# A hybrid block on one core: preparing the gate/up weights inside the output projection, and moving its token scale, its squares and the buffers of the down projection

## The chip, the core and the metric

One program runs on one core of a Trainium2 chip. The metric is device time in microseconds (us) of one execution, as a median of three. The engines named here are TensorE (PE in the profile), VectorE (DVE), ScalarE (ACT), GpSimd (POOL) and SyncE (SP), which issues most transfers (DMA). PSUM is the memory into which matmuls write; SBUF holds everything else.

## The reference

For 512 tokens, a model width of 2048 and an inner width of 5632 (all float32):

```
mod = silu(c) @ w_ada + b_ada -> sh1, sc1, g1, sh2, sc2, g2
u   = rmsnorm(h) * norm_attn * (1 + sc1) + sh1
y   = concat(FoX heads, NSA heads)(u @ w_in) @ w_out     # mixer
h   = h + g1 * y
u   = rmsnorm(h) * norm_ffn * (1 + sc2) + sh2
h   = h + g2 * ((silu(u @ w_gate) * (u @ w_up)) @ w_down)
out = rmsnorm(h) * final_norm
```

The change touches the end of `@ w_out`, the second norm, the start of gate/up, the passage to `@ w_down`, and the last norm.

## The kernel before, in words

The hidden state stays transposed: 16 tiles `hT` of 128 features x 512 tokens. Every large product is computed from split operands. A raw weight `wr` is rounded to `wh` on ACT (L239), the rest `wl` is formed on DVE (L240), and PE adds three matmuls, high x high, low x high and high x low (L255 to L257). One `gemm` goes through its weights in chunks `ct` and calls a `hook(ct)` after the matmuls of each chunk.

The output projection runs in groups of feature tiles; the last two are tiles 10 to 13 and tiles 14 and 15. The latter has eight chunks of 12 matmuls. After a group, `res_add` forms `hT` on DVE (L1006), ACT squares it (L997), POOL adds the squares up (L999), and `sum_rstd` sums over the features with 128x1 matmuls on PE (L821): of the running sum `hsum` and of the last two squares. `rstd_of` makes the inverse root on DVE and ACT; `rows_of` spreads it over the partitions with four matmuls (L173), and ACT copies the result into the SBUF tile `rb` (L175).

Gate and up together are 176 steps `s` (22 groups of 8 steps). A step multiplies seven combinations of two activation tiles with seven of the weights, in 42 matmuls of 128x256 into seven PSUM banks `y`. For its weights it needs `raw` (two loads on SP), the sums `sum` (DVE), and the splits `hx`/`lx` and `hs`/`ls`: `hx`, `hs` and a first form of `lx` on ACT, `ls` on DVE, while the second half of `lx` is an adding transfer that POOL issues (L1039). For its activations, in the first eight steps alone, DVE scales two `hT` tiles by the norm (`u_raw`, L1053, with `rb`), DVE or POOL takes differences (`u_mix`, L1059 to L1062), ACT rounds (`uh`), and DVE forms the rests (`ul`, L1076 and L1079). After a group, `evac` combines the seven banks on DVE (L1109 to L1115), and `glu` sends the product to DRAM (`hd`).

The down projection reads `hd` back (`hr`, L1254), splits it into `fh` (ACT) and `fl` (DVE, L1258), and runs four phases over the inner width, each of four groups of four feature tiles. Its SBUF pools lie over those of gate/up, so each tile waits until the old tiles at its address are dead. In the last phase the squares of the new `hT` (called `hU` there) are added up as above. The tail transposes `hU` (L1294), scales it into `ot` (L1297 and L1299), and stores it (L1300) from four buffers.

The order on each engine comes from a scheduler, except from the first `u_raw` to the last `evac`, where program order holds on every engine. Each engine works its queue in order, so an instruction that waits holds all behind it. SP always follows program order.

Of the kernel before, what the change touches and what calls it, by code (L numbers as in the profile page):

```python
# [13 lines left out]
OP = mybir.AluOpType  # L14
# [63 lines left out]
def hymba_block(ctx: ExitStack, tc: tile.TileContext, x, c, positions, w_ada, b_ada, norm_attn,  # L78
# [738 lines left out]
    def sum_rstd(tiles, n, tag, name):  # L817
        b = bank(tag)
        for i, a in enumerate(tiles):
            for t in range(NT):  # L820
                nc.tensor.matmul(b[:, t:t + 1], a[:, t * P:(t + 1) * P], one_col, start=i == 0 and t == 0,  # L821
                                 stop=i == len(tiles) - 1, skip_group_check=True)
        return rstd_of(b[:, 0:NT], n, name)
# [163 lines left out]
    pf = pool(wo, "pf")  # L987
# [3 lines left out]
    def add_sq(src, i, acc, name):  # L991
        if i == 0:
            acc.append(pf.tile([P, T], F32, tag="osum", name=name))
            nc.scalar.activation(acc[0], src, AF.Square)
            return
        sq = pf.tile([P, T], F32, tag="sq", name=uid("sq"), bufs=3)
        nc.scalar.activation(sq, src, AF.Square)  # L997
        if i < ND - 2:
            nc.gpsimd.tensor_tensor(acc[0], acc[0], sq, op=OP.add)  # L999
        else:  # L1000
            acc.append(sq)
# [34 lines left out]
    def x_low(s):  # L1036
        lx[s] = ring2.tile([P, 3, HT], F32R, tag="lx", name=uid("lx"), bufs=4)
        nc.scalar.activation(lx[s], raw[s][:, 1:4, :], AF.Copy, scale=-1.0)  # L1038
        nc.gpsimd.dma_start(split_ap(lx[s]), raw[s][:, 1:4, :], accum_op=OP.add)  # L1039

    def s_split(s):
        hs[s] = ring2.tile([P, 4, HT], F32R, tag="hs", name=uid("hs"), bufs=2)
        ls[s] = ring2.tile([P, 4, HT], F32R, tag="ls", name=uid("ls"), bufs=2)
        nc.scalar.copy(hs[s], sums[s])  # L1044
        nc.vector.tensor_tensor(ls[s], sums[s], split_ap(hs[s]), op=OP.subtract)  # L1045
# [80 lines left out]
    hsum = []  # L1126
    side_ada.extend(ada_block(pf, sec, j) for sec, j in todo_ada[9:])
    for i0, n, g in ((0, 4, g0), (4, 2, g1), (6, 4, BANKS_A), (10, 4, BANKS_B), (14, 2, BANKS_A)):
        k0 = 8 if i0 < 6 else 0
        if i0 >= 6:  # L1130
            g = out_group(i0, n, g)

        def x_hook(ct):
            if ct == k0 // 2 + 2:
                for i in range(i0, i0 + n):
                    nc.sync.dma_start(hT[i], xsp[i])

        gemm(*g, order=order, k0=k0, hook=x_hook, n_ada=1)
        res_add(i0, [o[3] for o in g[3]], 2, hsum, "hsum")
        for i in range(i0, i0 + n):  # L1140
            nc.gpsimd.dma_start(hsd[i], hT[i])
    pump(side_ada, 1000)
    for s in range(6):
        w_load(s)
# [3 lines left out]
    for s in range(2):  # L1148
        w_sums(s)
    for s in range(2):  # L1150
        x_high(s)
    rb = rows_of(sum_rstd(hsum, D, "mm", "rs2"), "mm", res.tile([P, T], F32, name="rb2"))
# [37 lines left out]

    u_raw(0)
# [3 lines left out]
    for s in range(3):  # L1195
        x_low(s)
    s_split(0)
# [42 lines left out]
    hp = pool(ft, "hp", reuse_waits="tile")  # L1240
    hT = [hp.tile([P, T], F32, name=f"hU{i}") for i in range(ND)]
# [3 lines left out]
    fsum = []  # L1245
# [6 lines left out]
    def h_tile(i):  # L1252
        r = pf.tile([P, T], F32, tag="hr", name=uid("hr"), bufs=4)
# [15 lines left out]
    for p, ph in enumerate(phases):  # L1269
# [3 lines left out]
        for g in range(4):  # L1273
            Z = banks4()

            def hook(ct):
                if p == 0 and ct == 2:
                    for i in range(4 * g, 4 * g + 4):
                        nc.sync.dma_start(hT[i], hsd[i])
                if nxt and (ct % 2 or nk < 12):  # L1280
                    b.append(h_tile(nxt.pop(0)))
# [5 lines left out]
    rf = sum_rstd(fsum, D, "mm", "rs3")  # L1287
    for i in range(ND):
        nc.scalar.activation(hT[i], hT[i], AF.Copy, scale=fin[:, i:i + 1])
    for t in range(NT):  # L1290
        for g in range(4):
# [3 lines left out]
            ot = pf.tile([P, T], F32, tag="hr", name=uid("ot"), bufs=4)  # L1295
# [31 lines left out]
```

## Time and profile before

| | before |
|---|---|
| median of 3 runs | 2497.86 us (2496.89 to 2498.45) |
| the profiled execution | 2492.28 us, of which the span is 2490.4 us |
| mean granted clock of TensorE | 0.969 of full |
| busy: PE, DVE, ACT, POOL | 94%, 66%, 42%, 18% |
| chain that ended last | PE 53%, DVE 1%, DMA 1% |

The profiled execution lies 5.6 us below the median of the runs, and 1.9 us of it lie outside the span. The rows below count from the start of the span. PE is busy nearly throughout; the stretches beside the change in which it isn't are the passage from the output projection to gate/up (from about 1046 us), the passage to the down projection (from about 1968 us), and the tail (from about 2468 us).

### The profile page before, as it was taken

The numbers are of one execution on the slowest core, as the hardware profiler recorded it, in microseconds if no ns is written. First come the engines' busy times: TensorE is split into PE (matmuls) and PEld (weight loads), VectorE is DVE, ScalarE is ACT, GpSimd is POOL, SyncE is SP. The second block draws the span as 40 slices with busy tenths as digits, with TensorE's granted clock in tenths as the row PEclk, the third lists the DMA queues.
The fourth block names the chain that finished last, engine by engine and source line by source line (L and its number), as shares of the span: only waits on it lengthen the run. The fifth ranks groups of instructions, "written<-read, shape, count | busy, mean of one in ns | idle before, by whom it ended". The sixth has DMA issues, their size and how long they took to land.

```text
span 2490.4 us, 38618 instructions
## 1 busy us (share of the span) xinstructions
PE 2336.9 (94%) x14643; PEld 2094.0 (84%) x14643; DVE 1633.2 (66%) x2757; ACT 1055.0 (42%) x1619; POOL 458.1 (18%) x468
## 2 busy tenths in 40 slices
PE   4688999999999989879999999999999799999998
PEld 3576888788887768769999999999999788888887
DVE  8995787887755565597777777777776533333333
ACT  4343643433423332355555555555555322222233
POOL 5564000200010221162221212222221100000011
PEclk7798999999999999989999999999999899999998
DMA  9782653453655267559898889898988454333322
GB/s 299 237 263 90 195 154 127 124 152 114 193 154 159 81 218 251 178 137 222 225 224 217 220 213 239 215 226 212 223 200 196 129 188 134 126 119 119 106 93 102
DMA packets 321690, 440.31 MB, mean 177 GB/s; under 512 B 25200, under 2 KB 216528, under 8 KB 321504
## 3 DMA queue, kind: packets, MB, share of 16 engines
q1 hardware_dynamic: 288080, 348.20, 43.4%
q0 software_dynamic: 31120, 85.45, 18.4%
q10 hardware_dynamic: 2304, 4.20, 0.4%
q8 instruction: 115, 1.88, 0.3%
q14 instruction: 71, 0.58, 0.1%
HBM read 340.18 MB, written 28.38 MB: 148 GB/s over the span
## 4 chain that ended last, share of the span: by engine, by line
PE 53%; DVE 1%; DMA 1%; ACT 0%; issue 0%; POOLq 0%; POOL 0%; SPq 0%; DVEq 0%; ACTq 0%
PE py L1096 11%; PE py L1099 11%; PE py L1098 11%; PE psmm L256 3%; PE psmm L257 3%; PE psmm L255 3%; PE pss L255 2%; PE pss L256 2%; PE pss L257 2%; PE pso L256 1%; PE pso L257 1%; PE pso L255 1%; DMA wr<-in_w_down_dram 0%; DMA out_dram<-ot 0%; DVE ot L1297 0%
## 5 line engine op out<-in xcount | busy, mean ns | idle before, releaser
L240 DVE TENSOR_TENSOR wl<-wr,wh 128x1024 fp32r<-128x1024 f32 (+2 forms) x194 | 219.5, 1132 | 366.9 <-ACT wh L239 365.2
L239 ACT CAST wh<-wr 128x1024 fp32r<-128x1024 f32 (+2 forms) x210 | 199.0, 948 | 514.4 <-PE psmm L256 212.7
L1099 PE MATMUL py<-uh,ls 128*128 128x256 f32 x1408 | 398.4, 283 | 3.0 <-DVE ls L1045 3.0
L1098 PE MATMUL py<-ul,hs 128*128 128x256 f32 x1408 | 399.0, 283 | 1.5 <-DVE ul L1079 1.5
L1096 PE MATMUL py<-uh,hs 128*128 128x256 f32 x1408 | 399.5, 284 | 1.0 <-DVE ev L1113 0.5
L1044 ACT CAST hs<-sum 128x1024 fp32r<-128x1024 f32 x176 | 184.5, 1048 | 383.5 <-PE py L1098 257.2
L1045 DVE TENSOR_TENSOR ls<-sum,hs 128x1024 fp32r<-128x1024 f32 x176 | 215.3, 1224 | 195.3 <-ACT hs L1044 195.3
L1098 PE MATMUL py<-ul,hx 128*128 128x256 f32 x1056 | 297.4, 282 | 8.3 <-DVE ul L1079 8.3
L1099 PE MATMUL py<-uh,lx 128*128 128x256 f32 x1056 | 298.0, 282 | 6.2 <-DMA lx<-raw 6.2
L1096 PE MATMUL py<-uh,hx 128*128 128x256 f32 x1056 | 299.3, 283 | 2.3 <-ACT uh L1078 2.0
L1099 PEld LDWEIGHTS py<-uh,ls 128*128 128x128 f32 x1408 | 269.0, 191 | 4.0 <-DVE ls L1045 3.8
L1096 PEld LDWEIGHTS py<-uh,hs 128*128 128x128 f32 x1408 | 268.3, 191 | 2.6 <-issue 0.7
L1098 PEld LDWEIGHTS py<-ul,hs 128*128 128x128 f32 x1408 | 268.4, 191 | 2.3 <-DVE ul L1079 2.3
L1039 POOL DMA_DIRECT2D lx<-raw x176 | 155.9, 891 | 552.8 <-ACT lx L1038 385.0
L1098 PEld LDWEIGHTS py<-ul,hx 128*128 128x128 f32 x1056 | 199.4, 189 | 9.4 <-DVE ul L1079 9.4
L1099 PEld LDWEIGHTS py<-uh,lx 128*128 128x128 f32 x1056 | 199.4, 189 | 6.5 <-DMA lx<-raw 6.5
L1096 PEld LDWEIGHTS py<-uh,hx 128*128 128x128 f32 x1056 | 200.3, 190 | 2.8 <-ACT uh L1078 2.3
L358 DVE SCALAR_TENSOR_TENSOR acc<-ad,sl,acc 128x512 f32<-128x512 f32 x180 | 140.0, 778 | 51.4 <-DMA ad<-in_w_ada_dram 49.8
L1038 ACT ACTIVATE lx<-raw 128x768 fp32r<-128x768 f32 x176 | 148.0, 842 | 0.0
L1034 ACT CAST hx<-raw 128x768 fp32r<-128x768 f32 x176 | 144.0, 818 | 1.7 <-DMA raw<-in_w_gate_dram 1.7
L255 PE MATMUL psmm<-fh,wh 128*128 128x512 f32 x352 | 136.9, 389 | 0.0
L256 PE MATMUL psmm<-fl,wh 128*128 128x512 f32 x352 | 136.9, 389 | 0.0
(438 smaller groups left out, 5481.3 us busy)
## 6 DMA issues: line engine op xcount, KB each, us to landing
ad<-in_w_ada_dram SPq DMA_DIRECT2D x192, 512.0 KB, 4.7
lx<-raw POOLq DMA_DIRECT2D x176, 384.0 KB, 4.9
raw<-in_w_up_dram SPq DMA_DIRECT2D x176, 256.0 KB, 4.1
raw<-in_w_gate_dram SPq DMA_DIRECT2D x176, 256.0 KB, 4.3
wr<-in_w_down_dram SPq DMA_DIRECT2D x88, 512.0 KB, 3.7
wr<-in_w_in_dram SPq DMA_DIRECT2D x104, 256.0 KB, 3.7
wr<-in_w_in_dram SPq DMA_DIRECT2D x24, 512.0 KB, 4.4
wr<-in_w_out_dram SPq DMA_DIRECT2D x24, 512.0 KB, 4.7
```

Source lines behind the costliest of these rows:

```text
L239: nc.scalar.copy(wh[:, :, s], v)
L240: lo.tensor_tensor(wl[:, :, s], v, split_ap(wh)[:, :, s], op=OP.subtract)
L255: nc.tensor.matmul(dst, wh[:, k, w], ah, start=first, stop=False)
L256: nc.tensor.matmul(dst, wh[:, k, w], al, start=False, stop=False)
L257: nc.tensor.matmul(dst, wl[:, k, w], ah, start=False, stop=last)
L1038: nc.scalar.activation(lx[s], raw[s][:, 1:4, :], AF.Copy, scale=-1.0)
L1039: nc.gpsimd.dma_start(split_ap(lx[s]), raw[s][:, 1:4, :], accum_op=OP.add)
L1044: nc.scalar.copy(hs[s], sums[s])
L1045: nc.vector.tensor_tensor(ls[s], sums[s], split_ap(hs[s]), op=OP.subtract)
L1096: nc.tensor.matmul(o, wh[:, wi, js], vh[:, vi, :], start=k == 0 and j == 0, stop=False, skip_group_check=True)
L1098: nc.tensor.matmul(o, wh[:, wi, js], vl[:, vi, :], start=False, stop=False, skip_group_check=True)
L1099: nc.tensor.matmul(o, wl[:, wi, js], vh[:, vi, :], start=False, stop=k == KG - 1, skip_group_check=True)
```

## The change

It has five parts. (a) The hook of the last `w_out` group issues the loads of the first six weight steps, the sums and `hx` of steps 0 and 1, `lx` of steps 0 to 2 and `hs` of step 0; `lx` and `hs` move to the pool `ring1`, which exists by then. (b) The spread token scale `rb` stays in a PSUM bank of gate/up, where `u_raw` reads it; the copy on ACT goes. (c) `s_split(0)`, which forms `ls` of step 0, stands ahead of `u_raw(0)`. (d) The tiles of the squares in the down stage move to the pool `hp`, and `hr` and `ot` have eight buffers for four; the addresses of the down stage's other buffers shift by this, over other tiles of gate/up. (e) POOL adds up fewer squares of the last norm (tiles 0 to 11 for 0 to 13); their sum goes to PE in the middle of the last group, and each remaining square has its own matmuls (`sum_tok`). For the second norm POOL's sum goes to PE inside the last group likewise.

```diff
@@ -814,8 +814,8 @@
                 nc.gpsimd.tensor_tensor(osum[grp][0], osum[grp][0], sq, op=OP.add)
         return f
 
-    def sum_rstd(tiles, n, tag, name):
-        b = bank(tag)
+    def sum_rstd(tiles, n, tag, name, b=None):
+        b = bank(tag) if b is None else b
         for i, a in enumerate(tiles):
             for t in range(NT):
                 nc.tensor.matmul(b[:, t:t + 1], a[:, t * P:(t + 1) * P], one_col, start=i == 0 and t == 0,
@@ -984,21 +984,26 @@
     rs = ExitStack()
     res = pool(rs, "res", side="right", reuse_waits="tile")
     wo = ExitStack()
-    pf = pool(wo, "pf")
+    pf = sqp = pool(wo, "pf")
     hT = [res.tile([P, T], F32, name=f"hT{i}") for i in range(ND)]
     hsd = [dram.tile([P, T], F32, name=f"hsd{i}") for i in range(ND)]
 
     def add_sq(src, i, acc, name):
         if i == 0:
-            acc.append(pf.tile([P, T], F32, tag="osum", name=name))
-            nc.scalar.activation(acc[0], src, AF.Square)
+            acc["t"] = sqp.tile([P, T], F32, tag="osum", name=name)
+            nc.scalar.activation(acc["t"], src, AF.Square)
             return
-        sq = pf.tile([P, T], F32, tag="sq", name=uid("sq"), bufs=3)
+        sq = sqp.tile([P, T], F32, tag="sq", name=uid("sq"), bufs=3)
         nc.scalar.activation(sq, src, AF.Square)
-        if i < ND - 2:
-            nc.gpsimd.tensor_tensor(acc[0], acc[0], sq, op=OP.add)
+        if i < acc["n"]:
+            nc.gpsimd.tensor_tensor(acc["t"], acc["t"], sq, op=OP.add)
         else:
-            acc.append(sq)
+            sum_tok(acc, sq, False, i == ND - 1)
+
+    def sum_tok(acc, a, first, last):
+        for t in range(NT):
+            nc.tensor.matmul(acc["b"][:, t:t + 1], a[:, t * P:(t + 1) * P], one_col, start=first and t == 0,
+                             stop=last, skip_group_check=True)
 
     def res_add(i0, Z, sec, acc, name):
         for m in range(len(Z)):
@@ -1034,14 +1039,18 @@
         nc.scalar.copy(hx[s], raw[s][:, 1:4, :])
 
     def x_low(s):
-        lx[s] = ring2.tile([P, 3, HT], F32R, tag="lx", name=uid("lx"), bufs=4)
+        lx[s] = ring1.tile([P, 3, HT], F32R, tag="lx", name=uid("lx"), bufs=4)
         nc.scalar.activation(lx[s], raw[s][:, 1:4, :], AF.Copy, scale=-1.0)
         nc.gpsimd.dma_start(split_ap(lx[s]), raw[s][:, 1:4, :], accum_op=OP.add)
 
+    def s_high(s):
+        hs[s] = ring1.tile([P, 4, HT], F32R, tag="hs", name=uid("hs"), bufs=2)
+        nc.scalar.copy(hs[s], sums[s])
+
     def s_split(s):
-        hs[s] = ring2.tile([P, 4, HT], F32R, tag="hs", name=uid("hs"), bufs=2)
+        if s not in hs:
+            s_high(s)
         ls[s] = ring2.tile([P, 4, HT], F32R, tag="ls", name=uid("ls"), bufs=2)
-        nc.scalar.copy(hs[s], sums[s])
         nc.vector.tensor_tensor(ls[s], sums[s], split_ap(hs[s]), op=OP.subtract)
 
     V, tmix, ur = {}, {}, {}
@@ -1123,7 +1132,7 @@
         nc.gpsimd.dma_start(hd[g][:, :, 0:HT], u1)
         nc.gpsimd.dma_start(hd[g][:, :, HT:], u2)
 
-    hsum = []
+    hsum = {"n": 14}
     side_ada.extend(ada_block(pf, sec, j) for sec, j in todo_ada[9:])
     for i0, n, g in ((0, 4, g0), (4, 2, g1), (6, 4, BANKS_A), (10, 4, BANKS_B), (14, 2, BANKS_A)):
         k0 = 8 if i0 < 6 else 0
@@ -1134,22 +1143,29 @@
             if ct == k0 // 2 + 2:
                 for i in range(i0, i0 + n):
                     nc.sync.dma_start(hT[i], xsp[i])
+            if i0 == 14:
+                if ct < 6:
+                    w_load(ct)
+                if ct == 2:
+                    hsum["b"] = bank("s")
+                    sum_tok(hsum, hsum["t"], True, False)
+                if 2 <= ct < 4:
+                    w_sums(ct - 2)
+                    x_high(ct - 2)
+                if 2 <= ct < 5:
+                    x_low(ct - 2)
+                if ct == 5:
+                    s_high(0)
 
         gemm(*g, order=order, k0=k0, hook=x_hook, n_ada=1)
         res_add(i0, [o[3] for o in g[3]], 2, hsum, "hsum")
         for i in range(i0, i0 + n):
             nc.gpsimd.dma_start(hsd[i], hT[i])
     pump(side_ada, 1000)
-    for s in range(6):
-        w_load(s)
     scale_vec(1, 0, ND)
     dsh = con.tile([P, KG], F32, name="dsh")
     nc.vector.tensor_tensor(dsh, mod[:, 3 * ND + KG:4 * ND], mod[:, 3 * ND:3 * ND + KG], op=OP.subtract)
-    for s in range(2):
-        w_sums(s)
-    for s in range(2):
-        x_high(s)
-    rb = rows_of(sum_rstd(hsum, D, "mm", "rs2"), "mm", res.tile([P, T], F32, name="rb2"))
+    r2 = rstd_of(hsum["b"][:, 0:NT], D, "rs2")
     pk.close()
     wo.close()
     aw.close()
@@ -1188,13 +1204,14 @@
         m0 = 5 * ND + 2 * j
         nc.vector.tensor_tensor(mod[:, m0:m0 + 2], b[:, 0:2], b_mod[:, m0:m0 + 2], op=OP.add)
 
+    rb = ps2.tile([P, T], F32, tag="y", name=uid("py"), bufs=8)
+    for t in range(NT):
+        nc.tensor.matmul(rb[:, t * P:(t + 1) * P], r2[:, t:t + 1].to_broadcast([P, P]), ident, start=True, stop=True)
+    s_split(0)
     u_raw(0)
     u_mix(0, nc.vector)
     u_raw(1)
     u_mix(1, nc.gpsimd)
-    for s in range(3):
-        x_low(s)
-    s_split(0)
     u_split(0)
     u_raw(2)
     late = []
@@ -1238,11 +1255,12 @@
     fs.close()
     ft = ExitStack()
     hp = pool(ft, "hp", reuse_waits="tile")
+    sqp = hp
     hT = [hp.tile([P, T], F32, name=f"hU{i}") for i in range(ND)]
     wts = pool(ft, "wts2", reuse_waits="tile")
     pf = pool(ft, "pf2", reuse_waits="tile")
     phases = [range(0, 12), range(12, 24), range(24, 36), range(36, 44)]
-    fsum = []
+    fsum = {"n": 12}
     which = [0]
 
     def banks4():
@@ -1250,7 +1268,7 @@
         return [bank(t) for t in (BANKS_B if which[0] else BANKS_A)]
 
     def h_tile(i):
-        r = pf.tile([P, T], F32, tag="hr", name=uid("hr"), bufs=4)
+        r = pf.tile([P, T], F32, tag="hr", name=uid("hr"), bufs=8)
         nc.sync.dma_start(r, hd[i // 2][:, i % 2, :])
         h = pf.tile([P, T], F32R, tag="fh", name=uid("fh"), bufs=24)
         l = pf.tile([P, T], F32R, tag="fl", name=uid("fl"), bufs=24)
@@ -1277,6 +1295,9 @@
                 if p == 0 and ct == 2:
                     for i in range(4 * g, 4 * g + 4):
                         nc.sync.dma_start(hT[i], hsd[i])
+                if p == 3 and g == 3 and ct == 2:
+                    fsum["b"] = bank("o")
+                    sum_tok(fsum, fsum["t"], True, False)
                 if nxt and (ct % 2 or nk < 12):
                     b.append(h_tile(nxt.pop(0)))
 
@@ -1284,7 +1305,7 @@
                  hook=hook, first=w_first if p == 0 and g == 0 else None)
             res_add(4 * g, Z, 5, fsum if p == 3 else None, "fsum")
         a = b
-    rf = sum_rstd(fsum, D, "mm", "rs3")
+    rf = rstd_of(fsum["b"][:, 0:NT], D, "rs3")
     for i in range(ND):
         nc.scalar.activation(hT[i], hT[i], AF.Copy, scale=fin[:, i:i + 1])
     for t in range(NT):
@@ -1292,7 +1313,7 @@
             b = bank(tags[(t * 4 + g) % 8])
             for i in range(4):
                 nc.tensor.transpose(b[:, i * P:(i + 1) * P], hT[4 * g + i][:, t * P:(t + 1) * P], ident)
-            ot = pf.tile([P, T], F32, tag="hr", name=uid("ot"), bufs=4)
+            ot = pf.tile([P, T], F32, tag="hr", name=uid("ot"), bufs=8)
             if g % 2:
                 nc.vector.tensor_scalar(ot, b, rf[:, t:t + 1], None, op0=OP.mult)
             else:
```

What stands where on the engines is shown for the places of which the prediction speaks. First DVE at the end of the output projection, from the last weight rest of the group of tiles 10 to 13 (`wl_9502` is the first one of the last group; L1011 is L1006 of before):

```order
 L240 TENSOR_TENSOR wl_9446<-wr_9443,wh_9445 128x1024
+L1032 TENSOR_TENSOR sum_9575<-raw_9523 128x512
+L1033 TENSOR_TENSOR sum_9575<-sum_9575,raw_9523 128x256
+L1034 TENSOR_TENSOR sum_9575<-sum_9575,raw_9523 128x256
+L1032 TENSOR_TENSOR sum_9605<-raw_9544 128x512
+L1033 TENSOR_TENSOR sum_9605<-sum_9605,raw_9544 128x256
+L1034 TENSOR_TENSOR sum_9605<-sum_9605,raw_9544 128x256
 L240 TENSOR_TENSOR wl_9502<-wr_9499,wh_9501 128x2x256
-L1006 SCALAR_TENSOR_TENSOR hT_8579<-pss_9190,mod,hT_8579 128x512
+L1011 SCALAR_TENSOR_TENSOR hT_8579<-pss_9190,mod,hT_8579 128x512
```

Six sums of the first two weight steps now stand ahead of the weight rest with which the last group begins, and of the four residual adds.

ACT at the same place, after the change (`wh_9501` and `wh_9528` are the first two rounded weights of the last group):

```order
L239 CAST wh_9445<-wr_9443 128x1024 [waits DMAHW4_49,DVE_49,PE_49]
L1039 CAST hx_9579<-raw_9523 128x768 [waits DMAHW7_49,DMAHW0_49]
L1043 ACTIVATE lx_9581<-raw_9523 128x768
L1048 CAST hs_9659<-sum_9575 128x1024 [waits DVE_49]
L1039 CAST hx_9609<-raw_9544 128x768 [waits DMAHW3_49,DMAHW2_49]
L239 CAST wh_9501<-wr_9499 128x2x256 [waits DMAHW6_49,PE_49,Activation_49]
L1043 ACTIVATE lx_9611<-raw_9544 128x768
L997 ACTIVATE sq_9478<-hT_8579 128x512 [waits DVE_49,Pool_49]
L1043 ACTIVATE lx_9635<-raw_9567 128x768 [waits DMAHW7_49,DMAHW0_49]
L997 ACTIVATE sq_9482<-hT_8580 128x512 [waits DVE_49,Pool_49]
L997 ACTIVATE sq_9486<-hT_8581 128x512 [waits DVE_49,Pool_49]
L239 CAST wh_9528<-wr_9526 128x2x256 [waits DMAHW1_49,PE_49,Activation_49]
```

The two rounded weights stand behind copies that wait for the raw loads of steps 0, 1 and 2; before, none of the L1039, L1043 and L1048 rows was there.

DVE at the start of the down stage, after the change (`py` are the banks of the last gate/up group):

```order
L240 TENSOR_TENSOR wl_20874<-wr_20871,wh_20873 128x1024 [waits DMAHW0_49,Activation_49]
L1276 TENSOR_TENSOR fl_20880<-hr_20877,fh_20879 128x512 [waits DMASW7_49,DMAHW1_49,DMASW5_49,Activation_49]
L1276 TENSOR_TENSOR fl_20886<-hr_20883,fh_20885 128x512 [waits DMASW3_49,DMASW4_49,DMASW2_49,DMASW6_49,DMASW1_49,DMASW7_49,DMASW0_49,DMAHW2_49,PE_49,Activation_49]
L1276 TENSOR_TENSOR fl_20892<-hr_20889,fh_20891 128x512 [waits DMAHW3_49,Activation_49]
L1276 TENSOR_TENSOR fl_20898<-hr_20895,fh_20897 128x512 [waits DMASW3_49,DMAHW4_49,DMASW1_49,Activation_49]
L1118 TENSOR_TENSOR ev_20902<-ev_20901,py_20431 128x512 [waits Activation_49]
L1276 TENSOR_TENSOR fl_20927<-hr_20924,fh_20926 128x512 [waits DMAHW5_49,Activation_49]
L1119 TENSOR_TENSOR ev_20901<-ev_20901,py_20438 128x512 [waits DVE_49]
L1276 TENSOR_TENSOR fl_20933<-hr_20930,fh_20932 128x512 [waits DMAHW6_49,Activation_49]
L1120 TENSOR_TENSOR ev_20903<-ev_20901,py_20445 128x512 [waits DVE_49]
L1276 TENSOR_TENSOR fl_20939<-hr_20936,fh_20938 128x512 [waits DMAHW7_49,Activation_49]
L1121 TENSOR_TENSOR ev_20901<-ev_20901,py_20452 128x512 [waits DVE_49]
```

The second `fl` waits for PE: its address is that of an `lx` tile which the last matmul of gate/up reads. Before, it had no wait for PE. The next row, L1122, is the last reader of the bank into which the first matmul of down writes.

PE in the tail, after the change, from the last matmul of the down stage:

```order
L257 MATMUL psmm_23852<-fh_23174,wl_23951 128x512
L1005 MATMUL pso_23943<-cs,sq_23979 128x1 x4
L1005 MATMUL pso_23943<-cs,sq_23986 128x1 x4
L1315 MATMUL psmm_24032<-cs,hU_20849 128x128
L1005 MATMUL pso_23943<-cs,sq_23993 128x1 x4
L1315 MATMUL psmm_24032<-cs,hU_20850 128x128
```

and ten more L1315 ahead of the fourth set of squares (`sq_24000`). Before, `fsum` and two sets of squares stood there, with two and ten transposes between them.

## Rows read from the trace of the kernel before

**Rows 1.** Window: us; busy PE, PEld, DVE, ACT, POOL; clock; DMA share; GB/s.

```profile
1080.00:1090.00 10.00, 7.54 (x57) 6.93 (x57) 9.86 (x14) 4.86 (x8) 7.62 (x7) 1.00 0.41 95
```

**Rows 2.** Timeline of PE from the last output matmul: start, us, ..., [idle before <-releaser].

```profile
1045.50 0.39 PE L257 MATMUL psmm<-yh,wl 128*128 128x512 f32 x1
...
1048.08 1.05 PE L821 MATMUL psmm<-cs,sq 128*128 128x1 f32 x8 [0.51 <-ACT sq L997]
...
1050.50 2.07 PE L173 MATMUL psmm<-cs,rs2r 128*128 128x128 f32 x8 [1.36 <-DVE rs2r L167]
...
1066.32 0.58 PE L1099 MATMUL py<-uh,lx 128*128 128x256 f32 x1 [6.25 <-DMA lx<-raw]
```

**Rows 3.** ACT, the copy of the token scale, in the timeline.

```profile
1052.61 0.59 ACT L175 COPY rb<-psmm 128x512 f32<-128x512 f32 x1 [2.10 <-PE psmm L173]
```

**Rows 4.** DVE at the start of gate/up, in the timeline.

```profile
1053.23 1.42 DVE L1053 SCALAR_TENSOR_TENSOR hT<-hT,a_vec,rb 128x512 f32<-128x512 f32 x2 [2.79 <-ACT rb L175]
...
1057.35 1.22 DVE L1045 TENSOR_TENSOR ls<-sum,hs 128x1024 fp32r<-128x1024 f32 x1
...
1058.48 2.08 DVE L1079 SCALAR_TENSOR_TENSOR ul<-hT,mod,uh 128x256 fp32r<-128x256 f32 x2
...
1062.48 0.47 DVE L1079 SCALAR_TENSOR_TENSOR ul<-tmix,mod,uh 128x256 fp32r<-128x256 f32 x1
```

**Rows 5.** Line L1053 alone: its busy time in a window, then its forms.

```profile
1053.00:1131.00 78.00, 15.49 (x16) 0.88 0.56 129
...
L1053 DVE SCALAR_TENSOR_TENSOR ur<-hT,a_vec,rb x6: 1219/1224/1230, 1082.2 to 1099.9; 128x512 f32<-128x512 f32 x6
```

**Rows 6.** DVE and POOL side by side in the last output groups, in the timeline.

```profile
1020.50 0.75 DVE L1006 SCALAR_TENSOR_TENSOR hT<-pss,mod,hT 128x512 f32<-128x512 f32 x1 [0.61 <-PE pss L257]
...
1020.77 1.30 POOL L999 TENSOR_TENSOR hsum<-hsum,sq 128x512 f32<-128x512 f32 x1
```

**Rows 7.** The last output group: ACT, a window, a transfer's KB and landing, lx's queue.

```profile
1026.66 0.62 ACT L239 CAST wh<-wr 128x512 fp32r<-128x512 f32 x1 [1.97 <-PE psmm L256]
...
1022.00:1028.00 6.00, 6.00 (x32) 5.08 (x31) 5.36 (x6) 2.40 (x4) 5.45 (x7) 1.00 0.57 207
...
raw<-in_w_up_dram SPq DMA_DIRECT2D x6, 256.0 KB, 5.6
...
q0 software_dynamic: 296, 0.82, 76.1%
```

**Rows 8.** PE and one window at the start of the down stage.

```profile
1968.36 0.28 PE L1099 MATMUL py<-uh,lx 128*128 128x256 f32 x1
...
1981.34 0.77 PE L255 MATMUL pss<-fh,wh 128*128 128x512 f32 x1 [12.70 <-DVE ev L1114]
...
1993.08 0.79 PE L255 MATMUL pss<-fh,wh 128*128 128x512 f32 x1 [3.97 <-ACT wh L239]
...
1980.00:1985.00 5.00, 3.66 (x9) 2.92 (x10) 5.00 (x9) 1.91 (x4) 1.46 (x2) 0.50 0.42 136
```

**Rows 9.** DVE in the same place, first and last of seven starts.

```profile
1976.68 0.68 DVE L1109 TENSOR_TENSOR ev<-ev,py 128x512 f32<-128x512 f32 x1
...
1980.52 0.68 DVE L1114 TENSOR_TENSOR ev<-ev,py 128x512 f32<-128x512 f32 x1
```

**Rows 10.** SP in the same place, the loads of the down stage.

```profile
1968.37 16.82 SPq L1254 DMA_DIRECT2D hr<-hd  x12
```

**Rows 11.** PE at the end of the down stage and in the tail.

```profile
2467.39 0.39 PE L256 MATMUL psmm<-fl,wh 128*128 128x512 f32 x1
...
2467.61 0.39 PE L257 MATMUL psmm<-fh,wl 128*128 128x512 f32 x1
...
2472.29 1.71 PE L821 MATMUL psmm<-cs,sq 128*128 128x1 f32 x8
```

**Rows 12.** DVE, the first output tile.

```profile
2475.34 1.41 DVE L1297 TENSOR_SCALAR ot<-psmm,rs3r 128x512 f32<-128x512 f32 x2
```

**Rows 13.** SP, the stores of the output.

```profile
2476.12 11.46 SPq L1300 DMA_DIRECT2D out_dram<-ot  x16
```

## The prediction

> **What bounds the kernel now.** I read the 40 slices of the page first: PE is busy nearly throughout, so the trace matters where it isn't, and of those places the change touches three. The windows and PE's timeline show what ends the waits there.
>
> Into gate/up. From the last output matmul (1045.50 + 0.39 = 1045.89 [rows 2]) to the first `u_raw` at 1053.23 [rows 4] a chain of 7.3 us runs with PE mostly idle. Then DVE is the limit: from 1080 to 1090 it is busy for 9.86 of 10 us and PE for 7.54 [rows 1]. PE's largest single wait, 6.25 us for `lx` [rows 2], is therefore not worth 6.25: with `lx` there, PE waits for the next thing that DVE makes. What counts is DVE's start and its work.
>
> Into down. The last gate/up matmul ends at 1968.64, the first of down starts at 1981.34, behind the combination L1114 [rows 8]; 3.97 us more are lost before 1993.08, behind a rounded weight. PE restarts at half clock, 0.50 granted, 1.2 for 2.4 GHz [rows 8].
>
> In the tail, from 2468.00 [rows 11] on, the order of the sums and then the stores decide.
>
> **Part by part, gate/up.** (1) The square of tile 15 no longer stands behind copies for `lx`: the 0.51 us wait for it [rows 2] and the set of the POOL sum leave the end. PE then has two sets of 1.05 us, the last once the square is there: residual add 0.75 [rows 6], square some 0.6 (an ACT pass over such a tile takes 0.59 [rows 3]), set 1.05, together 2.4 after the last matmul, for 3.2 now (1048.08 + 1.05 = 1049.13). That saves 0.8. The steps to `rows_of` stay (1.36 us, then 2.07 [rows 2]), and `u_raw` reads PSUM without the copy of 0.59 [rows 3], which saves 0.6. Sum: −1.4.
>
> (2) The POOL sum's set now lies between matmuls of the last output group, where PE is full: +1.0, a set's 1.05.
>
> (3) The last output group gets in-order neighbours. Now the rounded weight of its second chunk runs at 1026.66, in time for PE [rows 7]. After, it stands behind copies that wait for raw tiles 1 and 2, and the weight rest of the first chunk behind the sums. Tile 2 can be issued at about 1019 to 1020 (SP's order, behind the same weight load as now), and such tiles land after 5.6 us when six go together [rows 7]: copy, two squares and rounding then end at about 1027.5 to 1028.5, for 1026.7 plus the little slack that PE has. Transfers are also moved into a busier stretch: in 1022 to 1028 the DMA share is 0.57 already [rows 7], and three `lx` need about 4.6 us of all engines for 0.82 of their 1.18 MB (76.1% of 6 us [rows 7]), so some 6.5 us for all. I take +2.0, an estimate between 0 (everything lands early) and +5 (backlog of raw and `lx`, which reaches the later weights).
>
> (4) `ls` of step 0, 1.22 us of DVE [rows 4], moves into the time in which DVE waits for the token scale: −1.2. If `hs` came late, the cover would be gone and the 1.2 be paid again.
>
> (5) `u_raw` itself. Its 16 instructions take 15.49 us [rows 5]; beside POOL's `u_mix` one takes 1.22 [rows 5], two in a free stretch 1.42, so 0.71 each [rows 4]. An add of the same shape with one operand in PSUM takes 0.75 with POOL at work beside it [rows 6]. Taking 0.75 for all, 12.0 us: −3.5. The bounds are 0 (the 1.22 stay, or another DVE operation waits instead) and −5, if POOL also gets faster.
>
> The Trainium skill ("SBUF — State Buffer", section “SBUF: two separate sides”) says that DVE and GpSimd share a port pair as an exclusive lock, asked for by a DVE operation with two SBUF inputs against a GpSimd operation that reads SBUF, and that the loser blocks for the whole instruction. Rows 5 and 6 agree on who is slowed; by the lock, though, the next two-operand DVE operation would inherit the wait. That speaks against (5), and the first rival below prices it from rows.
>
> DVE carries (4) and (5) at their full size since it is the bound. Sum for gate/up: −1.4 + 1.0 + 2.0 − 1.2 − 3.5 = −3.1.
>
> **Down.** Now the loss against matmuls in a row is 12.70 + 3.97 [rows 8], plus the half-clock restarts: nine matmuls in 3.66 us [rows 8] are 0.41 each for 0.22 (2467.61 − 2467.39 [rows 11]), some ten after the first gap (2.0) and six or seven after the second (1.4). Sum 20.1. After, the first weight and eight `hr` no longer lie over tiles that the last step uses; the waits in SP's order point to matmuls three to six steps earlier, so they land with time to spare. The 12 `hr` issues that now hold SP for 16.82 us [rows 10], with the second weight behind them, have buffers. Now PE has that weight 7.9 us after it can be issued (1993.08 − 1985.19 [rows 8, 10]). After, it is issued about 2.5 us behind the end of gate/up (four `fl` at 0.64, below, free what it queues behind), so it is there at about +10.4, and up to 3 later where DVE's queue holds its rest. PE wants it after the first chunk, at 9.1 (below) + 24 matmuls × 0.22 = +14.4. The 3.97 and the 1.4 go, with 1 to 4 us to spare.
>
> The first gap doesn't go. The second `fl` now lies over an `lx` that the last matmul reads, and DVE's queue holds all of `evac` behind it. Eleven DVE operations, up to the one that frees the first bank, follow that matmul. Six starts take 3.84 us now [rows 9], 0.64 each: 7.0, with the hand-over 7.1. A gap of that size should cost the half clock too, since 3.97 us did [rows 8]: +2.0. Loss 9.1 for 20.1: −11.0. Bounds: −13 if the clock doesn't fall, −5.6 if the second weight is late as now.
>
> **Tail.** POOL's sum goes to PE inside the last group: +1.0. After the last matmul PE now has two sets and two plus ten transposes before the last set, which ends at 2474.00 (2472.29 + 1.71 [rows 11]), 6.0 after 2468.00. After, three sets, one transpose and eleven more come before the fourth: about 1.05 × 2 + 0.2 + 1.05 to 1.7 + 2.4 + 1.7 = 7.5 to 8.1, +1.8 at the middle. The first output tile [rows 12] shifts by this. Eight output buffers save some of DVE's and ACT's waits for the stores, but those are spread over 11.5 us [rows 13] and mostly run at the transfer's rate: −0.7, between 0 and −1.4. Sum +2.1.
>
> **Total**: −3.1 − 11.0 + 2.1 = −12.0. On the profiled execution that is 2492.28 − 12.0 = 2480.3; the median of the runs is 5.6 above that execution, and the forecast goes from it: 2497.86 − 12.0 = 2485.9, say 2486.
>
> **Rivals.** A, the contention only moves. POOL still runs 7.62 of 10 us [rows 1], and the wait that `u_raw` loses is met by the next DVE operation with two SBUF operands, `ul` or `ls`. For it: two `ul` take 2.08 together where one alone takes 0.47 [rows 4]. Against: what is slowed has both operands in SBUF, and `u_raw` was such a taker more. Without (5): 2486 + 3.5 = 2489.5.
>
> B, the change doesn't do what it says at the down stage: a wait of a load or a split I took for early is for the last step, or the eleven operations are joined by others. Then 20.1 stay: 2486 + 11 = 2497. Against it stand the waits in the order.
>
> C, slower. In the last output group SP issues each weight behind two raw loads, and ACT and DVE take weights only behind raw work. If weights and raw tiles queue up in the transfers, each of eight chunks starves PE. It takes 12 us more than my 2.0, 1.75 a chunk, to lose the whole gain, and 17 to be slower by 0.2%. At 2.6 a chunk (21 us) the time is 2505. Against: the transfers stand at about half load, and three weight buffers are some 8 us of matmuls.
>
> D, more than I take. If POOL, freed of `u_raw`, ends its work earlier, the pair of `ul` falls from 2.08 towards twice 0.47, and similar operations with it: about 2 us in each of five steps, 10: 2476. Against: DVE's order keeps them beside `u_mix`.
>
> **Chances.** Forecast 0.62 (its own range 2480 to 2491, from (3), (5) and the tail's bounds), A 0.13, B 0.09, C 0.06, D 0.10. The range takes in A and most of D: 2476 to 2494; B and C, 0.15, stay out. About 0.2% (5 us) is what a measurement of this kernel can tell from no change. Faster by more: forecast, A and D nearly whole, 0.83; within: B and a bit of A, 0.11; slower: C, 0.06.
>
> **What would show it.** Windows after the last output matmul: `u_raw` starting about 6 us behind it, its forms at 0.75 beside POOL, and the DVE-bound stretch some 3 us shorter or more. In the last output group, PE waits for rounded weights of about 2 us in all. At down, a first gap near 7 us ended by L1122, and no second gap. In the tail, the last set of squares 7.5 to 8 us after the last matmul. A first gap of 12, `u_raw` still at 1.22, or waits over 5 us in the output group would prove a step wrong.

## The result, and the profile after

The changed kernel takes 2482.41 us (median of four runs, 2476.54 to 2482.58), against 2498.15 for the kernel before: a ratio of 0.9932 (95% interval 0.9915 to 0.9949), 15.7 us faster, where 12.0 were forecast. Executions of one kernel differ by several us before they reach the change's place: in the profile of before the first output matmul starts at 837.32, after at 843.54, with the same code ahead of it. The spans therefore say less than the stages, which I take from the traces between the ends of matmuls: the output stage (first to last output matmul), gate/up (from there to its last matmul), down (to its last matmul), and the tail (to the end of the span).

| us | before | after | difference | forecast |
|---|---|---|---|---|
| output stage | 208.6 | 213.3 | +4.7 | +3.0 |
| gate/up, its start included | 922.8 | 913.6 | −9.1 | −6.1 |
| down, its start included | 499.4 | 488.6 | −10.8 | −10.0 |
| tail | 22.4 | 21.6 | −0.8 | +1.1 |
| sum | 1653.1 | 1637.1 | −16.0 | −12.0 |

First the last output group after the change: DVE, PE and ACT in the timeline, then two windows with the columns of [rows 1].

```profile
1028.19 0.69 DVE L1032 TENSOR_TENSOR sum<-raw 128x512 f32<-128x512 f32 x1 [1.95 <-DMA raw<-in_w_gate_dram]
...
1030.32 2.06 DVE L1011 SCALAR_TENSOR_TENSOR hT<-pss,mod,hT 128x512 f32<-128x512 f32 x3
...
1031.12 1.05 PE L362 MATMUL pss<-cs,acc 128*128 128x1 f32 x8 [1.12 <-DVE hT L1011]
...
1033.59 0.84 ACT L1043 ACTIVATE lx<-raw 128x768 fp32r<-128x768 f32 x1 [1.80 <-DMA raw<-in_w_gate_dram]
...
1028.00:1034.00 6.00, 4.88 (x22) 3.81 (x21) 4.85 (x9) 3.14 (x5) 3.25 (x4) 0.84 1.01 273
1034.00:1040.00 6.00, 6.00 (x24) 4.63 (x23) 3.18 (x3) 3.67 (x7) 4.89 (x5) 0.88 1.09 290
```

DVE waits 1.95 us for the raw tile of step 1, so the residual adds come late, and PE waits 1.12 for the bank that they free. After this short wait the windows grant only 0.84 and 0.88 of the clock, where PE had 1.00 before [rows 7]. ACT waits for the raw tile of step 2, as forecast, but it was DVE's queue that held PE first. Counted from the end of the group of tiles 10 to 13, the last group takes 26.85 us for 22.71 before, so that 4.1 of the stage's 4.7 arise in it.

The start of gate/up, PE and DVE in the timeline, then the lines that answer to [rows 5]:

```profile
1056.46 0.39 PE L257 MATMUL psmm<-yh,wl 128*128 128x512 f32 x1
1057.05 1.05 PE L1005 MATMUL pss<-cs,sq 128*128 128x1 f32 x8 [0.21 <-ACT sq L997]
1058.41 1.05 PE L1005 MATMUL pss<-cs,sq 128*128 128x1 f32 x8 [0.31 <-ACT sq L997]
1060.83 2.08 PE L1209 MATMUL py<-cs,rs2r 128*128 128x128 f32 x8 [1.36 <-DVE rs2r L167]
...
1057.55 1.22 DVE L1054 TENSOR_TENSOR ls<-sum,hs 128x1024 fp32r<-128x1024 f32 x1
...
1062.95 1.41 DVE L1062 SCALAR_TENSOR_TENSOR hT<-hT,a_vec,py 128x512 f32<-128x512 f32 x2 [2.17 <-PE py L1209]
...
1067.05 1.72 DVE L1088 SCALAR_TENSOR_TENSOR ul<-hT,mod,uh 128x256 fp32r<-128x256 f32 x2
...
1087.78 1.39 DVE L1062 SCALAR_TENSOR_TENSOR ur<-hT,a_vec,py 128x512 f32<-128x512 f32 x2
1089.09 1.14 DVE L1088 SCALAR_TENSOR_TENSOR ul<-hT,mod,uh 128x256 fp32r<-128x256 f32 x2
...
1095.03 1.40 DVE L1062 SCALAR_TENSOR_TENSOR ur<-hT,a_vec,py 128x512 f32<-128x512 f32 x2
...
1091.71 2.24 POOL L1068 TENSOR_TENSOR tmix<-ur 128x256 f32<-128x256 f32 x1 [0.79 <-DVE ul L1088]
...
1095.68 0.74 POOL L1071 TENSOR_TENSOR tmix<-tmix,ur 128x256 f32<-128x256 f32 x1
...
1062.00:1142.00 80.00, 11.09 (x16) 0.91 0.53 126
...
L1062 DVE SCALAR_TENSOR_TENSOR ur<-hT,a_vec,py x6: 734/736/737, 1087.8 to 1103.0; 128x512 f32<-128x512 f32 x6
```

From the last output matmul (1056.85) to the first `u_raw` it is 6.1 us now, and `ls` of step 0 lies in that time. The 16 `u_raw` take 11.09 us for 15.49, each 0.74 beside POOL. Did their wait move on to the next operation? In a late step the pair of `ul` takes 1.14 and POOL's first difference 2.24. In the kernel before, the rows of the same steps read:

```profile
1082.22 2.37 DVE L1053 SCALAR_TENSOR_TENSOR ur<-hT,a_vec,rb 128x512 f32<-128x512 f32 x2
1084.51 1.14 DVE L1079 SCALAR_TENSOR_TENSOR ul<-hT,mod,uh 128x256 fp32r<-128x256 f32 x2
...
1090.47 2.37 DVE L1053 SCALAR_TENSOR_TENSOR ur<-hT,a_vec,rb 128x512 f32<-128x512 f32 x2
...
1087.13 2.25 POOL L1059 TENSOR_TENSOR tmix<-ur 128x256 f32<-128x256 f32 x1 [1.77 <-DVE ul L1079]
...
1091.11 1.18 POOL L1062 TENSOR_TENSOR tmix<-tmix,ur 128x256 f32<-128x256 f32 x1
```

The pair of `ul` and the first difference are as long as they were, so nothing was passed on. POOL's last difference, which runs beside `u_raw`, even falls from 1.18 to 0.74. From one pair of `u_raw` to the next it is 7.25 us for 8.25: a step is shorter by the full gain of its pair, twice the difference of 1.22 and 0.74. The first pair of `ul` got shorter too, 1.72 for 2.08 [rows 4].

The start of down, PE, DVE and then ACT in the timeline, to be read against [rows 8, 9]:

```profile
1970.20 0.28 PE L1108 MATMUL py<-uh,lx 128*128 128x256 f32 x1
1977.42 0.76 PE L255 MATMUL pss<-fh,wh 128*128 128x512 f32 x1 [6.93 <-DVE ev L1122]
...
1984.64 0.39 PE L255 MATMUL pss<-fh,wh 128*128 128x512 f32 x1
...
1985.10 0.39 PE L257 MATMUL pss<-fh,wl 128*128 128x512 f32 x1
...
1970.58 1.89 DVE L1276 TENSOR_TENSOR fl<-hr,fh 128x512 fp32r<-128x512 f32 x3 [6.83 <-issue]
1972.39 0.68 DVE L1118 TENSOR_TENSOR ev<-ev,py 128x512 f32<-128x512 f32 x1
...
1976.59 0.68 DVE L1122 TENSOR_TENSOR ev<-py,ev 128x512 f32<-128x512 f32 x1
...
1982.60 1.22 DVE L240 TENSOR_TENSOR wl<-wr,wh 128x1024 fp32r<-128x1024 f32 x1
...
1979.89 1.05 ACT L239 CAST wh<-wr 128x1024 fp32r<-128x1024 f32 x1 [1.36 <-DMA wr<-in_w_down_dram]
```

The second `fl` starts 0.1 us after gate/up's last matmul (1970.48), the combination follows in turn, and PE starts 6.93 us after that matmul, behind L1122. No second gap follows. PE comes to the second chunk at 1984.64 and first reads the weight's rest at 1985.10. The rounded weight is there at 1980.94, 3.7 us ahead, and the rest at 1983.82, 1.3 us ahead.

The tail, PE, DVE and SP in the timeline, and three windows of two us:

```profile
2458.65 0.39 PE L257 MATMUL psmm<-fh,wl 128*128 128x512 f32 x1
2458.88 1.84 PE L1005 MATMUL pso<-cs,sq 128*128 128x1 f32 x16
2460.58 0.31 PE L1315 MATMUL psmm<-cs,hU 128*128 128x128 f32 x1
2460.72 0.95 PE L1005 MATMUL pso<-cs,sq 128*128 128x1 f32 x8
2461.54 1.94 PE L1315 MATMUL psmm<-cs,hU 128*128 128x128 f32 x11
2463.27 1.71 PE L1005 MATMUL pso<-cs,sq 128*128 128x1 f32 x8
...
2466.32 1.41 DVE L1318 TENSOR_SCALAR ot<-psmm,rs3r 128x512 f32<-128x512 f32 x2
...
2467.10 9.99 SPq L1321 DMA_DIRECT2D out_dram<-ot  x16
...
2459.00:2461.00 2.00, 2.00 (x22) 2.00 (x20) 0.75 (x1) 1.93 (x4) 0.00 (x0) 1.00 0.00 0
2461.00:2463.00 2.00, 2.00 (x17) 2.00 (x17) 0.00 (x0) 1.59 (x2) 0.00 (x0) 0.81 0.03 8
2463.00:2465.00 2.00, 2.00 (x12) 2.00 (x11) 0.00 (x0) 0.00 (x0) 0.00 (x0) 0.50 0.00 0
```

The last set ends at 2464.98, 5.9 us after the last matmul (2459.04), for 6.0 in the kernel before: two sets took 1.84 together, and the clock fell only in the window from 2461. The stores' issues spread over 9.99 us, 11.46 before [rows 13]; from the first output tile to the end it is 14.3 us for 15.1.

### The profile page after: what moved, and what is told of

Its sections match the earlier page's. It is cut to its first block, busy times and chain, and to the rows that moved or that the text cites. A ratio compares the mean times of both kernels' runs of the same rounds, so it can differ in the third digit from the quotient of the medians.

```text
span 2480.6 us, 38623 instructions
## 1 busy us (share of the span) xinstructions
PE 2345.2 (95%) x14659; PEld 2100.3 (85%) x14659; DVE 1626.7 (66%) x2757; ACT 1053.7 (42%) x1618; POOL 451.3 (18%) x466
## 4 chain that ended last, share of the span: by engine, by line
PE 53%; DVE 1%; issue 0%; ACT 0%; DMA 0%; SPq 0%; DVEq 0%; ACTq 0%
PE py L1105 11%; PE py L1108 11%; PE py L1107 11%; PE psmm L255 3%; PE psmm L257 3%; PE psmm L256 3%; PE pss L255 2%; PE pss L256 2%; PE pss L257 2%; PE pso L257 1%; PE pso L256 1%; PE pso L255 1%; PE pso L1005 0%; DVE ul L1088 0%; DVE ls L1054 0%
## 5 line engine op out<-in xcount | busy, mean ns | idle before, releaser
L1048 ACT CAST hs<-sum 128x1024 fp32r<-128x1024 f32 x176 | 184.7, 1049 | 379.6 <-PE py L1107 255.0
L1043 ACT ACTIVATE lx<-raw 128x768 fp32r<-128x768 f32 x176 | 147.9, 840 | 1.8 <-DMA raw<-in_w_gate_dram 1.8
L1039 ACT CAST hx<-raw 128x768 fp32r<-128x768 f32 x176 | 144.3, 820 | 5.5 <-DMA raw<-in_w_gate_dram 5.5
L257 PE MATMUL psmm<-fh,wl 128*128 128x512 f32 x352 | 136.9, 389 | 0.0
```

What stands on the lines that cost most here:

```text
L257: nc.tensor.matmul(dst, wl[:, k, w], ah, start=False, stop=last)
```

## The experiments

Each kernel's time is given as its ratio to runs of the kernel before on the same chip, with a 95% interval; all medians are of 4 to 7 runs. The stages, from one profiled execution of each, in the order of the table above:

| kernel | output | gate/up | down | tail | ratio |
|---|---|---|---|---|---|
| changed | 213.3 | 913.6 | 488.6 | 21.6 | 0.9932 (0.9915 to 0.9949) |
| e1, scale copied to SBUF | 216.8 | 918.9 | 489.0 | 21.1 | 0.9957 (0.9941 to 0.9974) |
| e2, before, scale in PSUM | 210.1 | 917.1 | 499.7 | 22.0 | 0.9973 (0.9959 to 0.9987) |
| e3, no early weights | 209.8 | 913.9 | 488.3 | 21.8 | 0.9916 (0.9902 to 0.9931) |
| e13, e3 with loads for nobody | 211.2 | 914.1 | 489.7 | 20.2 | 0.9912 (0.9894 to 0.9929) |
| e8, before, down buffers | 210.1 | 923.5 | 486.4 | 20.0 | 0.9931 (0.9915 to 0.9946) |
| e5, combination first | 216.2 | 914.2 | 488.3 | 21.9 | 0.9923 (0.9905 to 0.9941) |
| e6, last squares as before | 217.9 | 914.5 | 488.6 | 20.0 | 0.9925 (0.9908 to 0.9943) |
| e10, e5 and second weight early | 216.4 | 914.3 | 483.4 | 20.3 | 0.9912 (0.9895 to 0.9930) |
| e11, e3 and e10 | 211.7 | 913.8 | 485.3 | 20.3 | 0.9894 (0.9876 to 0.9912) |
| e12, e11 and third weight early | 212.0 | 913.7 | 481.3 | 20.3 | 0.9889 (0.9871 to 0.9907) |

**e1, the scale copied back.**

```diff
+    nc.scalar.copy(rb2, rb)
+    rb = rb2                       # SBUF tile of pool res
     s_split(0)
     u_raw(0)
     ...
```

> The changed kernel with one step back: the token scale is copied from PSUM into an SBUF tile, and u_raw reads that. Theory (POOL slows DVE only where both operands lie in SBUF): the 16 u_raw take 15 us again for 11.1, the six late ones 1.22 each for 0.74, the copy adds 0.6, and POOL's first difference of each step goes back from 0.7 to about 2 us; the time from the last output matmul to the last gate/up matmul grows by 5 to 8 us, and so does the total. Rival (what shortened this stage is the early weights, and the wait merely moves to the next operation): the same stage grows by at most 1.5 us.

The 16 `u_raw` take 15.96 us, and gate/up 5.2 more than in the changed kernel. The rival, which let the wait move on, is out. One part of the expectation missed: POOL's first differences go from 0.7 to 1.1 us in the first two steps alone, and in the later ones they take 2.24 in both kernels.

**e2, the scale in PSUM alone.**

```diff
-    rb = rows_of(sum_rstd(hsum, D, "mm", "rs2"), "mm", res.tile(...))
+    r2 = sum_rstd(hsum, D, "mm", "rs2")
...
+    rb = ps2.tile([P, T], F32, tag="y", name=uid("py"), bufs=8)
+    for t in range(NT):
+        nc.tensor.matmul(rb[...], r2[:, t:t + 1].to_broadcast([P, P]), ident, ...)
     u_raw(0)
```

> The kernel before with one part of the change alone: the token scale stays in a PSUM bank and u_raw reads it there. Theory: 5 to 7 us faster than before, all of it between the last output matmul and the last gate/up matmul (0.6 for the copy, 4.4 for the u_raw, the rest on operations beside POOL). Rival (the contention only moves on): about 1 us.

Gate/up takes 5.7 us less than before, as expected, with `u_raw` at 11.09 us in all.

```profile
1040.00:1145.00 105.00, 15.96 (x16) 0.92 0.52 135
```

```profile
1040.00:1145.00 105.00, 11.09 (x16) 0.90 0.67 167
```

These are the busy times of the `u_raw` line in the same window (us; busy DVE; clock; DMA share; GB/s), of e1 and then of e2. e1 differs from the changed kernel, and e2 from the kernel before, by the place of one operand and its copy alone: 15.96 for 11.09, and 11.09 for 15.49 [rows 5].

**e3, no early weights.**

```diff
             if i0 == 14:
-                if ct < 6:
-                    w_load(ct)
                 if ct == 2:
                     ...
-                if 2 <= ct < 4:
-                    w_sums(ct - 2)
-                    x_high(ct - 2)
-                ...
     pump(side_ada, 1000)
+    for s in range(6):
+        w_load(s)
...
+    # w_sums and x_high of 0, 1 and x_low of 0 to 2, ahead of rstd_of
```

> The changed kernel without its part (a): loads, sums, hx and lx of the first weight steps are issued behind the last output group, as before, while lx and hs stay in the earlier pool. Theory (the weights' work in the queues of DVE and ACT holds the last output group back): the output stage loses its wait of 1.1 us and the half-clock stretch behind it, 3 to 4 us in all, and the time into gate/up stays within 1.5 us, since lx has 8 us before it is wanted: 1.5 to 4 us faster than the changed kernel. Rival (the early weights are what shortens the start of gate/up): the start of gate/up loses 4 us or more, and the total is slower than the changed kernel.

The output stage takes 209.8 us, 3.5 less than in the changed kernel, and gate/up 913.9, the same. So by the stages part (a) gains nothing and costs some us; the ratios say the same, but their intervals overlap. In the five profiles with early weights (changed, e1, e5, e6, e10) the output stage takes 213.3 to 217.9 us, on the mean 216.1, in the four without (e3, e11, e12, e13) 209.8 to 212.0, on the mean 211.2: 5.0 us, the top end of what I had allowed it.

The last group alone, from the end of the one before it, tells the parts apart. It takes 22.71 us in the kernel before, in e2 and in e8, 23.66 to 23.98 in the four that have the set of the sums in it, and 26.85 to 29.76 in the five that have the early weights as well: 1.0 for the set and, on the mean, 4.8 for the weights. In each of the five PE waits for the residual add in this group, 1.1 to 2.8 us, and some window of 6 us behind it grants less than 0.8 of the clock; in none of the other seven does it wait so or leave the full clock. In e1 and e6 a second wait follows, of 2.17 and 2.46, for a rounded weight on ACT. That is the wait of the forecast; of e1:

```profile
1038.15 1.05 PE L362 MATMUL pss<-cs,acc 128*128 128x1 f32 x8 [1.43 <-DVE hT L1011]
...
1044.24 0.79 PE L255 MATMUL psmm<-yh,wh 128*128 128x512 f32 x1 [2.17 <-ACT wh L239]
```

**e13, loads for nobody.** Twelve loads of the same size stand where the early ones stood in SP's queue, into tiles that nobody reads; the rest is e3.

```diff
             if i0 == 14:
+                if ct < 6:
+                    spoil = ring1.tile([P, 4, HT], F32, tag="raw", ...)
+                    nc.sync.dma_start(spoil[:, 0:2, :], wu_v[:, :, ct, 0:HT])
+                    nc.sync.dma_start(spoil[:, 2:4, :], wg_v[:, :, ct, 0:HT])
```

> The changed kernel without the early weights, and in the last output group the same twelve loads at the same places of SP's queue, into tiles that nobody reads; the true loads come behind the group. It tells whether the transfers or the in-order queues of ACT and DVE hold the output stage back. Theory (the queues): the stage takes 209 to 212 us as without early weights. Rival (the transfers, which delay the output weights): 214 us or more, as in the changed kernel.

PE never waits in the last group, although the transfers are as dense as in the changed kernel; a window of the last group, columns as above:

```profile
1028.00:1034.00 6.00, 6.00 (x31) 5.03 (x30) 2.26 (x3) 1.69 (x3) 0.92 (x1) 1.00 1.07 384
```

So it is the work in the queues of DVE and ACT that holds the stage back, and not the twelve loads. The adding transfers of `lx` stand behind the group here as in e3, so their share alone is not tested.

**e8, the down buffers alone.** The kernel before with the down part of (d): `sqp = hp` for the squares, and eight buffers for `hr` and `ot`.

> The kernel before with the down stage's part alone: squares in the other pool, eight buffers for the loads and the output tiles; lx and hs stay where they were. Theory: by the order the first four fl no longer wait for gate/up's last matmul, but the sixth fh (ACT) does, with three of the combinations behind it: a first gap of about 4.5 us (12.7 before, 6.9 in the changed kernel, where the move of lx put an fl over the last step's lx), no second gap, and 12 to 15 us faster than before, the output tail included. Rival (the loads' landing sets the start and not these waits): a first gap of 7 us or more.

```profile
1980.01 0.62 ACT L1258 CAST fh<-hr 128x512 fp32r<-128x512 f32 x1 [2.33 <-PE py L1099]
...
1984.49 0.76 PE L255 MATMUL pss<-fh,wh 128*128 128x512 f32 x1 [4.52 <-DVE ev L1114]
```

The sixth `fh` waits on ACT for the last gate/up matmul, and the first gap is 4.52 us, as the order said. Without the move of `lx`, down starts 2.4 us earlier than in the changed kernel; 1.2 of that is left when the clock is back at full, but the restarts of kernels with the same gap of 6.93 differ by as much.

By the runs, e8 (0.9931) can't be told from the changed kernel (0.9932), although it has nothing of what gate/up gained; by the sum of the stages it is 2.9 us behind (1640.0 for 1637.1). What (b) and (c) give in gate/up is mostly taken back in the other three stages.

**e5, the combination first, and e10, the second weight early.**

```diff
-    w_first = load_w([cols(w_down, 0, 512)], 0)
-    a = [h_tile(i) for i in range(4)]
-    glu(*evac(NG - 1))
+    w_first = [load_w([cols(w_down, 0, 512)], 0)]
+    second = fetch_w([cols(w_down, 0, 512)], 1)      # e10 alone
+    a = [h_tile(0)]
+    last = evac(NG - 1)
+    a += [h_tile(i) for i in range(1, 4)]
+    w_first.append(second())                         # e10 alone
+    glu(*last)
```

Both edits are shown in one; in e5 `w_first` stays as it was.

> The changed kernel with one order turned round: the combination of the last gate/up group stands behind the first split tile of the down stage, not behind the first four. Theory (the second fl, which waits for gate/up's last matmul, holds the combination in DVE's queue): most of the combination then runs while the last step's matmuls end, and the first gap falls from 6.9 us to 1 to 2. The second weight is no earlier than before (ready some 13 us after the end of gate/up) and is now wanted some 7 us after it: a second gap of 4 to 6 us opens with a half-clock start behind it, and the total stays within 2 us of the changed kernel. Rival (something else, such as the landing of the loads, sets the start): the first gap stays at 5 us or more.

> The changed kernel with the combination behind the first split tile and the second weight of down loaded and split ahead of the further split tiles. Theory: the first gap is 1 to 2 us and the second 0 to 2, so the time from the last gate/up matmul to the last of down falls by 5 to 7 us against the changed kernel, and so does the total. Rival (ACT and DVE have too much to do there, and the split tiles come late in turn): less than 3 us.

PE in e5, the first start of down, the next wait, and the start of the second chunk:

```profile
1975.49 0.47 PE L255 MATMUL pss<-fh,wh 128*128 128x512 f32 x1 [0.32 <-DVE ev L1122]
...
1977.19 0.50 PE L256 MATMUL pss<-fl,wh 128*128 128x512 f32 x1 [0.53 <-DVE fl L1276]
...
1986.25 0.79 PE L255 MATMUL pss<-fh,wh 128*128 128x512 f32 x1 [4.22 <-ACT wh L239]
```

In e5 the first gap is 0.32 us, and a second of 4.22 opens: 488.3 us, no gain at all. What the changed kernel loses in the first gap it would lose in the second. With the second weight early (e10) the stage falls by 5.2, and waits of 1.17 and 0.53 us are left behind the second chunk.

**e6, the last squares as before.** `fsum = {"n": 14}`, and all its sums on PE behind the last matmul.

> The changed kernel with the last norm's squares summed as before: POOL adds up 14 of them, and the sums on PE all stand behind the last matmul. Theory (the sums cost what they take, wherever they stand, and the tail's time hangs on the clock): the down stage loses the 0.95 us set, and the tail keeps its length within 1 us; the total is 0 to 2 us faster than the changed kernel. Rival (the sum in the middle of the group shortens the tail): the tail, from the last matmul of down to the end, grows by 1.5 us or more.

Down and tail together are 1.5 us shorter than in the changed kernel, though down alone is not: against the changed kernel's matmuls those of e6 fall 1.0 us behind in the restart at half clock, and win 0.9 where the set of the sums was. But the tail hangs on the clock more than on the order. Where it stays at full, the last matmul to the first output tile takes 5.7 us in the old order (e6, e8) and 6.0 in the new (e10 to e13); where it falls, 6.8 to 7.6 in either. So the sums' place is worth 0.3 us there. The set costs what it takes, as the expectation's theory said, and the total is within its 0 to 2 us; the tail itself is 1.6 us shorter, not within 1, since the clock stayed at full.

**e11 and e12, what follows.** e11 is e3 with e10's order; e12 loads the third weight ahead of the split tiles' loads too.

```diff
+    w_first = [fetch_w([cols(w_down, 0, 512)], c) for c in range(3)]
+    w_split = [w_first[0]()]
     a = [h_tile(0)]
     last = evac(NG - 1)
     a += [h_tile(i) for i in range(1, 4)]
+    w_split.append(w_first[1]())
     ...
```

> The changed kernel without the early weights in the output group, with the combination behind the first split tile and the second weight of down early. Theory (both stages are independent): 8 to 11 us faster than the changed kernel, the sum of the two steps. Rival: less than 5.

> As the kernel before it in this study (no early weights, combination behind the first split tile, second weight early), and the third weight of down is loaded ahead of the split tiles' loads too. Theory (the small waits behind the third chunk come from that load, which queues behind twelve others): the waits of about 1.2 to 1.7 and 0.5 us there go, and with them any fall of the clock; from the last gate/up matmul to the last of down 480 to 482 us, for 483.4 to 485.3. Rival (DVE's work is what is late there): no change within 1 us.

e11's stages add up to 1631.2 us, 5.9 less than the changed kernel's 1637.1, short of the 8 to 11 expected; by the ratios it is 0.38%, some 9 us. Its output stage is 1.6 us shorter and not 5, since the changed kernel's own profile has the shortest of the five with early weights. Its down stage lost 2.0 us of e10's gain to a wait of 1.65 for the third weight and the clock behind it:

```profile
1986.15 0.50 PE L255 MATMUL pss<-fh,wh 128*128 128x512 f32 x1 [1.65 <-ACT wh L239]
...
1987.00:1992.00 5.00, 4.59 (x14) 3.66 (x15) 2.15 (x3) 1.56 (x2) 0.00 (x0) 0.66 0.97 361
```

In e12 both are gone, and down takes 481.3 us, 18.1 less than before. e12 is the fastest: 2474.46 us (2467.12 to 2475.10), 27 below the kernel before on its chip.

## Why the prediction was right, and where its sizes were off

- The token scale's chain, (1) and (4): 7.3 to 6.1 us, −1.2 for −1.4, and `ls` hidden. Right.
- The output group, (2) and (3): +3.0 forecast, +4.7 measured, of which +4.1 in the last group. The set cost the 1.0 that I gave it. The early work cost 3.1 in this kernel and 4.8 on the mean of five, for 2.0. The mechanism (PE's work behind raw work in in-order queues) is shown by e3 and e13; the size was too small. I priced one late rounding on ACT at 2.0, and that wait came in e1 and e6 alone. What ended PE's wait first was DVE, whose sums of step 1 stood ahead of four residual adds, and behind a wait of 1.1 us came a stretch at a lower clock that I hadn't counted.
- `u_raw`, (5): −3.5 forecast, −4.4 measured, and more with it. Most of the 0.9 is an error of mine: I set 16 lengths of 0.75 against the 15.49 of a window, in which neighbours' overlapping ends count once. The 16 lengths before add up to 16.2, and against these 0.75 gives −4.2. The terms measured give −1.2 − 1.2 − 4.4 = −6.8 of the −9.1; of the other 2.3 the trace assigns some 1.0 to `ul` in the first two steps (the first pair 0.36 shorter) and 0.5 to one sum, and the rest stays open. Rival D, 2 us a step, did not come: the late steps' `ul` are unchanged. Rival A is refuted by e1, e2 and the rows of the late steps, which come 1.0 us closer. The lock of the Trainium skill ("SBUF — State Buffer", section “SBUF: two separate sides”) agrees with who is slowed (1.22 with two operands in SBUF, 0.74 with one). That the next two-operand operation inherits the wait was my reading of it; the unchanged 1.14 of the pair of `ul` speaks against it.
- Down: a first gap of 6.93 for 7.1, ended by L1122 as said, and no second gap: −11.8 without the set of the sums for −11.0. Right, and B is refuted. The second weight was there at +10.5 for a forecast +10.4, and PE came to it at +14.2 for +14.4: 3.7 us to spare, and 1.3 for its rest, where I had said 1 to 4. e5 shows that this hangs on the first gap: without it the weight is 4.2 late.
- Tail: this step failed. I had three sets, twelve transposes and the last set end at 7.5 to 8.1 us after the last matmul; it was 5.9. The two sets took 1.7 for 2.1, the third 0.95 for 1.05 to 1.7, and the eleven transposes 1.6 for 2.4; the last took its 1.7. The transposes' price was one at half clock, and the clock fell later than that: at 1.00 to 2461 and 0.81 to 2463. The order itself costs 0.3 at full clock (e6). The stores' −0.7 were −0.8, in every kernel with eight buffers.

Together: +1.7 worse in the output stage, −3.0 better in gate/up, −0.8 in down and −1.9 in the tail, which is the 4 us between −12.0 and −16.0. C and its starvation of all eight chunks did not come.

## What to carry to other kernels

Where DVE is the limit and GpSimd works beside it, an operand of DVE in PSUM instead of SBUF can pay: here 16 instructions gave 5 to 6 us with the copy saved. Work prepared early is only free if nothing that PE needs stands behind it in the same queue: here a scheduler put it ahead of weights and residual adds, and it cost 3 to 6 us and gained nothing. Where one wait covers another (first gap and second weight), removing one alone gains nothing: e5 gained 0, e10 5 and e12 7.

## What was not expected

The clock in the tail is not a property of the order: with the same tail code it stayed at 1.00 in e10 and e12 and fell to 0.50 in the changed kernel and e3 some 3 us behind the last matmul, which makes the last sum 1.3 to 1.5 us later. And the same code ahead of the change took 837 to 849 us to the first output matmul in these profiles; most of the difference between before and after arose in the attention stage, from 520 to 640 us. Why is open in both cases.
